# Second weights of small experts in one pass, their gate and silu moved, conversions paced by a clock model: a two-layer decoder trunk on one core

## The chip, the core and the metric

The kernel runs on one core of a Trainium2 chip. The metric is device time in microseconds from one launch, the median of three runs; for the kernel before these took 1669.72, 1660.96 and 1666.87 us. A further execution was recorded by the profiler; every row below is from that one.

The engines: TensorE (PE, with its weight loads as PEld), VectorE (DVE), ScalarE (ACT), GpSimd (POOL) and SyncE (SP), which here only issues DMAs. Each works through its own queue in the order in which the program wrote it.

## The reference, cut to what matters

Two layers; in each an attention stage and then a mixture of experts. Only the second is touched:

```python
D_MODEL, SEQ, D_EXPERT = 1024, 512, 512      # 512 tokens
N_GROUPS, EXPERTS_PER_GROUP, TOP_K = 4, 4, 2 # 16 experts, 2 per token
def _hier_moe(x, w_group, b_group, w_expert, b_expert, w1, w3, w2):
    # top-1 group, then top-2 experts of that group; gate = softmax of the two times group weight
    ...
    def expert_block(args):
        xb, e = args
        h = jax.nn.silu(xb @ w1[e]) * (xb @ w3[e])
        return h @ w2[e]
    ...   # rows times gate, summed back into their tokens
```

All weights are float32: 6.29 MB for each expert (w1 and w3 of 1024 x 512, w2 of 512 x 1024), 100.7 MB for each layer, and all sixteen experts are read. Run on the inputs, the reference routes at most 87 tokens to one expert in layer 0 and at most 142 in layer 1.

## The kernel before

A Python planner emits the whole program. In the attention stage it chooses the next step from a table of costs; in the expert stage the order is written out by hand in the loop `for e in range(NE + 1)` near the end of `trunk`. Storage is three pools: 42 pages of 128 x 1024 floats, 12 half pages (pg) and 8 PSUM banks.

**Places and kinds.** Experts are ordered at run time by their number of tokens; the first `N_FIRST` places go to experts 0, 1, ... whatever their count, so that their weights can be asked for before the routing is known. Place e takes the expert of rank `RANK[e]`. A place has a kind:

- *wide* (128 slots): rows and weights are each split into a rounded part (`hi`, ACT) and the rest (`lo`, DVE), both in fp32r, and a product is three passes: hi x hi, hi x lo, lo x hi. A wide left operand has a hi page and a lo page.
- *half* (64 slots, for the seven smallest): the left operand carries the hi of 64 tokens in columns 0 to 63 and their lo in columns 64 to 127, so a product is two passes; the two halves of the output are added after it (`folded`: a copy by ACT, an addition by DVE).
- *raw* (128 slots, ranks in `RAW`): rows and weights stay float32, a product is one float32 pass, and the weight is used as it landed.

**Blocks.** A weight block is 512 KB, one page: w1 and w3 in four blocks of two row tiles, w2 in four blocks of one. A block of w1 or w3 is two products, a block of w2 two (one for each half of the 1024 output columns). `Stream.conv_to` turns a landed block into its two parts; for a block marked `whole` it does nothing. `use(i)` first converts up to `LOOK_AHEAD` blocks beyond block i. `used(i)` frees the block and calls `ws.pump`, which emits weight loads on SP as long as more than a reserve of pages is idle (`MOE_RESERVE`, and `EX_PAGES` more while the block lies up to `EX_FROM` before a mark in place 5). A load waits on SP until the page that it was given is free.

**One place e**, in the order written: w1 of e (four blocks, into bank h1); `silu` of h1; for e = `EX_ROWS` the transposes of the rows of a possible further block; `hidden_T` of the place before (four transposes, then hi and lo of the result); w3 of e, first two blocks; w2 of e - 1, four blocks; `gated` and `scatter` of e - 1 (GpSimd adds the rows to yd); `rows_T` for e + 1; `fetch` of the rows `ROWS` places ahead; w3 of e, last two blocks; the product of silu and h3 on DVE. For half places `silu` is four steps: copy and addition (`folded`), Silu, and a multiplication by the gate; `gated` then only folds.

**Further block.** An expert with more tokens than slots gets another block of 128, run under a condition at place 5 (`further_blocks`). Its rows are fetched at the end of place 2. In this data layer 0 has none and layer 1 has one; with the new places the counts are the same.

## Time and profile before

| | us |
|---|---|
| median of three runs | 1666.87 |
| the profiled execution | 1661.48 |
| its span, first to last instruction | 1659.7 |
| expert stage of layer 0, from the first product of place 0 to the last of place 15 | 457 to 778 |
| expert stage of layer 1 | 1272 to 1625 |

The two expert stages are 321 and 353 us of the span. Times in the views are from the start of the span. In a timeline a line is a run of like instructions: start, length, engine, out<-in, count, and in brackets how long the engine had been idle before it and what ended the wait. Names are the pools' (page, pg, bank) with the numbers left out, so a line is placed by its counts: four transposes are `hidden_T`, eight are `rows_T`; a raw product is recorded as two matmuls, a wide one as three, a half one as two. Every instruction carries line 247, the helper that records them.

### The profile page before, as it was taken

To read this page: it belongs to the slowest core of one execution; us is meant where nothing else is said; L and a number is where in the kernel's file an instruction comes from. 1 tells how busy PE (TensorE), PEld (TensorE's weight loads), DVE (VectorE), ACT (ScalarE), POOL (GpSimd) and SP (SyncE) were. 2 spreads that over 40 slices of the span, in tenths; PEclk is the share of its full clock that TensorE was granted. 3 is DMA by queue.
4 is the path that set the end of the run, shared out by engine and by line. 5 is a ranking of instruction groups with operands and counts; after the bars stand their busy time and mean duration, and the time that the engine had idled before them with its cause. 6 is when DMAs were issued, how large, how long until landed. Compare 5 with 4: busy or idle time off the path is not lost. (4 is left out here: it accounts for less than half of the span.)

```text
span 1659.7 us, 22603 instructions
## 1 busy us (share of the span) xinstructions
PE 1437.5 (87%) x7604; PEld 1165.7 (70%) x7604; DVE 1097.8 (66%) x1961; ACT 873.8 (53%) x1675; POOL 336.2 (20%) x387
## 2 busy tenths in 40 slices
PE   8999999989697898987799999989696978888974
PEld 7988778877665566565699977879584655566662
DVE  4745674475886579586865546645758765597786
ACT  5444455443356577585544434555423654586772
POOL 1511110330412211111422112002213121111112
PEclk9999998999798899998789999989797989899987
DMA  8202111354299999994330102206334999599933
GB/s 255 67 1 76 53 39 39 111 196 178 102 322 336 323 324 370 360 332 143 122 96 26 45 20 90 76 8 217 133 127 151 382 309 346 187 369 363 365 131 127
DMA packets 152447, 303.59 MB, mean 183 GB/s; under 512 B 21976, under 2 KB 45224, under 8 KB 152312
## 3 DMA queue, kind: packets, MB, share of 16 engines
q1 hardware_dynamic: 138680, 269.74, 45.9%
q0 software_dynamic: 12448, 32.13, 6.9%
q8 instruction: 64, 1.05, 0.3%
q14 instruction: 71, 0.58, 0.1%
q10 hardware_dynamic: 1184, 0.08, 0.1%
HBM read 284.14 MB, written 27.33 MB: 188 GB/s over the span
## 5 line engine op out<-in xcount | busy, mean ns | idle before, releaser
L247 PE MATMUL bank<-page,page 128*128 128x512 f32 (+5 forms) x4416 | 982.8, 375 | 51.8 <-DVE page L247 30.1
L247 PEld LDWEIGHTS bank<-page,page 128*128 128x128 f32 (+2 forms) x4416 | 747.2, 202 | 198.0 <-issue 42.1
L247 DVE TENSOR_TENSOR page<-page,page 128x1024 fp32r<-128x1024 f32 (+4 forms) x462 | 517.2, 1162 | 144.1 <-ACT page L247 135.1
L247 ACT ACTIVATE page<-page 128x1024 fp32r<-128x1024 f32 (+1 forms) x438 | 420.2, 1020 | 60.0 <-DMA page<-yd 15.7
L247 PE MATMUL bank<-page,pg 128*128 128x64 f32 (+1 forms) x1408 | 320.0, 373 | 56.3 <-ACT pg L247 45.8
L247 PEld LDWEIGHTS bank<-page,pg 128*128 128x128 f32 x1408 | 244.3, 207 | 127.6 <-ACT pg L247 53.6
L247 ACT ACTIVATE page<-bank 128x256 f32<-128x256 f32 (+8 forms) x251 | 120.6, 504 | 245.0 <-PE bank L247 182.0
L247 ACT ACTIVATE pg<-bank 128x256 f32<-128x256 f32 (+6 forms) x223 | 101.6, 469 | 212.6 <-PE bank L247 207.5
L247 POOL DMA_INDIRECT yd<-page,xidx x30 | 46.6, 1554 | 474.7 <-ACT page L247 229.1
L247 DVE TENSOR_TENSOR page<-bank,page 128x256 fp32r<-128x256 f32 (+3 forms) x134 | 75.1, 594 | 76.7 <-ACT page L247 76.6
L247 PE MATMUL bank<-cid,pg 128*128 128x128 f32 (+2 forms) x500 | 85.0, 288 | 35.6 <-ACT pg L247 20.3
L247 PE MATMUL bank<-cid,page 128*128 128x128 f32 (+1 forms) x608 | 87.9, 283 | 31.6 <-DMA page<-x1d,eix 18.4
L247 POOL TENSOR_TENSOR page<-pg,pg 128x256 f32<-128x256 f32 (+1 forms) x56 | 50.3, 911 | 267.2 <-DVE pg L247 215.9
L247 PEld LDWEIGHTS bank<-cid,page 128*128 128x128 f32 (+1 forms) x608 | 72.3, 144 | 44.6 <-issue 23.0
L247 PEld LDWEIGHTS bank<-cid,pg 128*128 128x128 f32 (+2 forms) x500 | 59.0, 148 | 54.5 <-ACT pg L247 26.1
L247 ACT ACTIVATE pg<-pg 128x256 f32<-128x256 f32 (+5 forms) x146 | 68.6, 477 | 52.2 <-DVE pg L247 48.5
L247 POOL TENSOR_TENSOR page<-page,page 128x1024 f32<-128x1024 f32 (+4 forms) x32 | 63.8, 1998 | 158.7 <-ACT page L247 72.5
L247 DVE TENSOR_TENSOR pg<-bank,pg 64x512 f32<-64x512 f32 (+6 forms) x87 | 49.5, 568 | 47.8 <-ACT pg L247 46.7
L247 POOL CAST page<-page 64x512 fp32r<-64x512 f32 x48 | 29.9, 623 | 137.5 <-ACT page L247 103.3
L247 DVE COPY pg<-bank 128x256 f32<-128x256 f32 (+3 forms) x73 | 35.2, 484 | 25.6 <-PE bank L247 25.3
L247 POOL MEMSET page<- 128x1024 f32 (+1 forms) x34 | 45.8, 1347 | 16.7 <-PE bank L247 16.7
L247 ACT ACTIVATE page<-bank,gslot 128x512 f32<-128x512 f32 (+1 forms) x36 | 24.4, 686 | 40.6 <-PE bank L247 40.6
(217 smaller groups left out, 990.5 us busy)
## 6 DMA issues: line engine op xcount, KB each, us to landing
page<-in_w_dram SPq DMA_DIRECT2D x396, 512.0 KB
page<-in_w_in_dram SPq DMA_DIRECT2D x64, 512.0 KB
page<-in_w_out_dram SPq DMA_DIRECT2D x16, 512.0 KB
x1d<-page SPq DMA_DIRECT2D x8, 512.0 KB
yd<-page SPq DMA_DIRECT2D x8, 512.0 KB
page<-yd SPq DMA_DIRECT2D x8, 512.0 KB
scr<-pg POOLq DMA_DIRECT2D x16, 132.0 KB, 2.0
pg<-scr POOLq DMA_DIRECT2D x16, 132.0 KB, 4.0
```

The costliest lines, as they stand in the source:

```text
L247: r = f(*args, **kw)
```

## The change

- The w2 of half places is marked `whole`. `hidden_T` of a half place then copies 64 float32 columns on ACT (no hi and lo), a product of its w2 is one float32 pass with a left operand of 64 columns, and `gated` scales 64 rows by the gate on ACT as for the others. The multiplication of the silu by the gate and the two folds of the output go.
- Silu of a half place is written behind `hidden_T` instead of ahead of it.
- `RAW` goes from ranks 0, 3 and 6 to rank 0: two places of each layer are wide instead.
- `N_FIRST` 3, with `RANK` to match: places 1 and 2 are both wide, 13 and 14 both half.
- Conversions: at least 2 blocks ahead, up to 10 as long as the planner's clock of DVE is less than 2000 ns past its clock of PE and seven pages are idle. Loads: at most 22 landed and not yet converted; reserve 8 more pages for 12 blocks before the mark.
- Rows are fetched two places ahead of their transposes instead of one, and the rows of the further block are transposed in place 4.

```diff
-EX_ROWS = 3
+EX_ROWS = 4
-ROWS = 2
-LOOK_AHEAD = 5
-N_FIRST = 2
-RANK = (0, 1, 9, 2, 10, 3, 11, 4, 12, 5, 13, 6, 14, 7, 15, 8)
+ROWS = 3
+LOOK_AHEAD = (2, 10)
+MOE_RAW = 22
+CONV_LAG = 2000.0
+N_FIRST = 3
+RANK = (0, 1, 2, 9, 3, 10, 4, 11, 5, 12, 6, 13, 7, 14, 15, 8)
-RAW = (0, 3, 6)
+RAW = (0,)
-EX_FROM = 5
+EX_FROM = 12
-EX_PAGES = 5
+EX_PAGES = 8
...
-            return ws.add(src, k, D // k, whole=KIND[e] == "raw")
+            return ws.add(src, k, D // k, whole=KIND[e] == "raw" or KIND[e] == "half" and w is w2)
...
-                th = pg([128, 4, 128], F32 if kind == "raw" else F32R),
+                th = pg([128, 4, n]),
...
-            if kind == "raw":
+            if kind == "wide":
+                halves(th, b, slice(0, 4))
+            else:
                 nc.scalar.activation(th[0], b, AF.Copy)
-            else:
-                halves(th, b, slice(0, 4))
...
         def quarter2(ys, ht, w, j):
+            m = ht[0].shape[2]
             for n in range(2):
-                product(ys[n], [a[:, j] for a in ht], [p[:, 0, n * 512:(n + 1) * 512] for p in w], j == 0, j == 3)
+                product(ys[n][0:m], [a[:, j] for a in ht], [p[:, 0, n * 512:(n + 1) * 512] for p in w], j == 0, j == 3)
...
             if kind == "half":
                 folded(sl[0:64], h1)
-                nc.scalar.activation(sl[0:64], sl[0:64], AF.Silu)
-                nc.scalar.activation(sl[0:64], sl[0:64], AF.Copy, scale=g)
...
-        def gated(ys, g, kind="wide"):
-            yo = page([128, D])
-            for n in range(2):
-                c = slice(512 * n, 512 * n + 512)
-                if kind == "half":
-                    folded(yo[0:64, c], ys[n])
-                else:
-                    nc.scalar.activation(yo[:, c], ys[n], AF.Copy, scale=g)
+        def gated(ys, g, n=128):
+            yo = page([n, D])
+            for i in range(2):
+                nc.scalar.activation(yo[:, 512 * i:512 * i + 512], ys[i][0:n], AF.Copy, scale=g[0:n])
...
         def use(i):
-            ws.conv_to(min(i + LOOK_AHEAD, moe_q[l, NE - 1, "w2"][3]))
+            top = moe_q[l, NE - 1, "w2"][3]
+            ws.conv_to(min(i + LOOK_AHEAD[0], top))
+            while (ws.conv_i <= min(i + LOOK_AHEAD[1], top) and plan.clock["DVE"] < plan.clock["PE"] + CONV_LAG
+                   and len(page_s.idle) >= 2 + MOE_RESERVE):
+                ws.conv_to(ws.conv_i)
             return ws.parts[i]
...
-        ws.limit = moe_q[l, NE - 1, "w2"][3] + 1
+        ws.limit, ws.max_raw = moe_q[l, NE - 1, "w2"][3] + 1, MOE_RAW
...
             ht = hidden_T(prev, KIND[e - 1]) if e else None
             if e < NE:
+                if KIND[e] == "half":
+                    nc.scalar.activation(sl[0:64], sl[0:64], AF.Silu)
                 use_13(e, "w3", h3, range(2))
```

The order on ACT in layer 0, where a wide place is followed by a half one. Before (place 10): conversions (page<-page), the copy of `folded` (pg_8521<-bank), Silu, the gate, and then the hi part of `hidden_T` (pg_8527).

```order
L247 ACTIVATE page_8501<-page_8123 128x1024
L247 ACTIVATE page_8511<-page_8133 128x1024
L247 ACTIVATE pg_8521<-bank_8476 64x512
L247 ACTIVATE pg_8521<-pg_8521 64x512
L247 ACTIVATE pg_8521<-pg_8521,gslot 64x512
L247 ACTIVATE pg_8527<-bank_8529 128x512
L247 ACTIVATE page_8536<-page_8143 128x1024
```

Now, at the same spot (place 9; the copy is pg_8343<-bank, the hi part pg_8347):

```order
L249 ACTIVATE page_8323<-page_8021 128x1024
L249 ACTIVATE page_8333<-page_8041 128x1024
L249 ACTIVATE pg_8343<-bank_8302 64x512
L249 ACTIVATE pg_8347<-bank_8349 128x512
L249 ACTIVATE pg_8343<-pg_8343 64x512
L249 ACTIVATE page_8361<-page_8053 128x1024
```

The hi part of `hidden_T` no longer stands behind the Silu, and the multiplication by gslot is gone.

The order on DVE at the same spots. Before: two folds of the output of place 8 (page_8425<-bank), two lo parts of `rows_T` (128x4x64), two conversions, the product with h3 of place 9 (pg_8338), four conversions, the addition of `folded` (pg_8521) and the lo part of `hidden_T` (pg_8528).

```order
L247 TENSOR_TENSOR page_8425<-bank_8374,page_8425 64x512
L247 TENSOR_TENSOR page_8433<-bank_8434,page_8433 128x4x64
L247 TENSOR_TENSOR page_8433<-bank_8441,page_8433 128x4x64
L247 TENSOR_TENSOR page_8455<-page_8097,page_8453 128x1024
L247 TENSOR_TENSOR page_8465<-page_8109,page_8463 128x1024
L247 TENSOR_TENSOR pg_8338<-pg_8338,bank_8340 128x512
L247 TENSOR_TENSOR page_8479<-page_8111,page_8477 128x1024
L247 TENSOR_TENSOR page_8493<-page_8113,page_8491 128x1024
L247 TENSOR_TENSOR page_8503<-page_8123,page_8501 128x1024
L247 TENSOR_TENSOR page_8513<-page_8133,page_8511 128x1024
L247 TENSOR_TENSOR pg_8521<-bank_8476,pg_8521 64x512
L247 TENSOR_TENSOR pg_8528<-bank_8529,pg_8527 128x512
```

Now:

```order
L249 TENSOR_TENSOR page_8263<-bank_8264,page_8263 128x4x64
L249 TENSOR_TENSOR page_8263<-bank_8271,page_8263 128x4x64
L249 TENSOR_TENSOR page_8291<-page_7969,page_8289 128x1024
L249 TENSOR_TENSOR pg_8177<-pg_8177,bank_8179 128x512
L249 TENSOR_TENSOR page_8305<-page_7983,page_8303 128x1024
L249 TENSOR_TENSOR page_8309<-page_7993,page_8307 128x1024
L249 TENSOR_TENSOR page_8325<-page_8021,page_8323 128x1024
L249 TENSOR_TENSOR page_8335<-page_8041,page_8333 128x1024
L249 TENSOR_TENSOR pg_8343<-bank_8302,pg_8343 64x512
L249 TENSOR_TENSOR pg_8348<-bank_8349,pg_8347 128x512
```

Ahead of the product with h3 (pg_8177) stands one conversion instead of two, and the folds are gone; between that product and the addition there are four conversions in both.

The order on SP at the end of the attention stage of layer 0. Before: the last weight loads of places 0 and 1, the eight stores of x1d and yd (four token tiles each), then the read of the routing order, behind which all other loads stand.

```order
L247 DMA page_4322<-in_w_dram 128x2x512
L247 DMA x1d_295<-page_3725 128x1024
L247 DMA yd_298<-page_3725 128x1024
L247 DMA x1d_295<-page_3723 128x1024
L247 DMA x1d_295<-page_3721 128x1024
L247 DMA yd_298<-page_3723 128x1024
L247 DMA x1d_295<-page_3719 128x1024
L247 DMA yd_298<-page_3721 128x1024
L247 DMA yd_298<-page_3719 128x1024
L581 TENSOR_LOAD order
```

Now, the end of that stretch, with the last five of twelve further loads:

```order
L249 DMA x1d_296<-page_3724 128x1024
L249 DMA yd_299<-page_3724 128x1024
L249 DMA page_4574<-in_w_dram 128x1024
L249 DMA x1d_296<-page_3722 128x1024
L249 DMA x1d_296<-page_3720 128x1024
L249 DMA page_4610<-in_w_dram 128x1024
L249 DMA page_4612<-in_w_dram 128x1024
L249 DMA page_4681<-in_w_dram 128x2x512
L249 DMA yd_299<-page_3722 128x1024
L249 DMA page_4686<-in_w_dram 128x2x512
L249 DMA yd_299<-page_3720 128x1024
L583 TENSOR_LOAD order
```

Twelve loads that do not need the order stand ahead of it, some of them between the stores.

## Rows read from the trace of the kernel before

**Rows 1.** The page: the span, and PE's busy time, share of the span and instructions.

```profile
span 1659.7 us, 22603 instructions
...
PE 1437.5 (87%) x7604; PEld 1165.7 (70%) x7604; DVE 1097.8 (66%) x1961; ACT 873.8 (53%) x1675; POOL 336.2 (20%) x387
```

**Rows 2.** The waits of PE in the expert stage of layer 0 (457 to 770 us): who waited for whom, us in total, times, the longest.

```profile
PE bank L247 <- ACT pg L247: 21.0, 7, 4.2
PE bank L247 <- DMA page<-x1d,eix: 9.5, 1, 9.5
PE bank L247 <- DMA page<-in_w_dram: 2.7, 1, 2.7
```

**Rows 3.** The same in the expert stage of layer 1 (1272 to 1620 us).

```profile
PE bank L247 <- ACT pg L247: 20.4, 7, 4.2
...
PE bank L247 <- DMA page<-x1d,eix: 8.9, 1, 8.9
```

**Rows 4.** The timeline of PE early in the expert stage of layer 0: w2 of the raw place 0 and the transposes after it; w2 of the wide place 1 and the transposes after it; the list and the transposes of the further block; w2 of the wide place 3 and the transposes after it.

```profile
480.13 7.03 PE L247 MATMUL bank<-page,pg 128*128 128x512 f32 x16
487.00 1.04 PE L247 MATMUL bank<-cid,page 128*128 128x128 f32 x8
...
499.62 7.63 PE L247 MATMUL bank<-page,pg 128*128 128x512 f32 x24 [2.90 <-ACT pg L247]
507.09 1.03 PE L247 MATMUL bank<-cid,page 128*128 128x128 f32 x8
...
509.87 0.44 PE L247 MATMUL bank<-pg,pg 128*128 128x1 bf16 x12
...
525.41 1.94 PE L247 MATMUL bank<-cid,page 128*128 128x128 f32 x8 [9.53 <-DMA page<-x1d,eix]
527.28 0.69 PE L247 MATMUL bank<-cid,pg 64*128 64x64 f32 x4
...
548.89 8.64 PE L247 MATMUL bank<-page,pg 128*128 128x512 f32 x24 [3.26 <-ACT pg L247]
557.37 1.04 PE L247 MATMUL bank<-cid,page 128*128 128x128 f32 x8
```

**Rows 5.** The timeline of PE around places 8 to 10 of layer 0: w2 of the half place 8, `rows_T`, the last w3 blocks of the wide place 9, w1 of the half place 10, its first w3 blocks, w2 of place 9, `rows_T`.

```profile
648.12 3.89 PE L247 MATMUL bank<-page,pg 128*128 128x512 f32 x16
651.86 1.03 PE L247 MATMUL bank<-cid,page 128*128 128x128 f32 x8
652.65 2.98 PE L247 MATMUL bank<-page,page 128*128 128x512 f32 x12
656.45 3.92 PE L247 MATMUL bank<-page,page 128*128 128x512 f32 x16 [0.83 <-DVE page L247]
...
660.57 2.10 PE L247 MATMUL bank<-page,page 128*128 128x512 f32 x8
666.83 7.62 PE L247 MATMUL bank<-page,pg 128*128 128x512 f32 x24 [4.16 <-ACT pg L247]
674.28 1.03 PE L247 MATMUL bank<-cid,page 128*128 128x128 f32 x8
```

**Rows 6.** The timeline of DVE in the same stretch: two folds and two lo parts of `rows_T`, two conversions, the product with h3 of place 9, four conversions, the addition of `folded`, the lo part of `hidden_T`.

```profile
654.79 1.94 DVE L247 TENSOR_TENSOR page<-bank,page 64x512 f32<-64x512 f32 x4
656.65 2.34 DVE L247 TENSOR_TENSOR page<-page,page 128x1024 fp32r<-128x1024 f32 x2
658.92 0.67 DVE L247 TENSOR_TENSOR pg<-pg,bank 128x512 f32<-128x512 f32 x1
659.52 4.62 DVE L247 TENSOR_TENSOR page<-page,page 128x1024 fp32r<-128x1024 f32 x4
664.06 0.68 DVE L247 TENSOR_TENSOR pg<-bank,pg 64x512 f32<-64x512 f32 x1
666.81 0.69 DVE L247 TENSOR_TENSOR pg<-bank,pg 128x512 fp32r<-128x512 f32 x1 [2.07 <-ACT pg L247]
```

**Rows 7.** The timeline of ACT in the same stretch: Silu of place 10, the multiplication by its gate, the hi part of `hidden_T` of place 9.

```profile
664.77 0.63 ACT L247 ACTIVATE pg<-pg 64x512 f32<-64x512 f32 x1 [3.76 <-DVE pg L247]
665.43 0.72 ACT L247 ACTIVATE pg<-pg,gslot 64x512 f32<-64x512 f32 x1
666.18 0.60 ACT L247 ACTIVATE pg<-bank 128x512 fp32r<-128x512 f32 x1
```

**Rows 8.** Stretches of layer 0, PE, PEld, DVE, ACT and POOL busy us (x instructions), granted TensorE clock, DMA share, GB/s: from w2 of place 5 to w2 of place 7, from there to w2 of place 9, and from w2 of place 13 to near the end of the stage.

```profile
592.00:629.20 37.20, 32.25 (x137) 23.11 (x137) 32.35 (x35) 29.88 (x39) 7.34 (x6) 1.00 1.04 374
629.20:666.80 37.60, 32.64 (x144) 25.62 (x144) 34.10 (x36) 30.78 (x40) 7.35 (x6) 0.95 1.03 371
...
740.30:775.00 34.70, 29.44 (x117) 23.08 (x118) 29.00 (x35) 24.85 (x30) 4.80 (x5) 0.84 0.25 67
```

**Rows 9.** The timeline of PE in layer 1: `rows_T` just ahead of the further block, and the first products behind it.

```profile
1388.60 1.04 PE L247 MATMUL bank<-cid,page 128*128 128x128 f32 x8
...
1425.70 7.38 PE L247 MATMUL bank<-page,page 128*128 128x512 f32 x24 [0.87 <-PEq L2094]
```

**Rows 10.** The timeline of SP (DMA issues) from 444 to 461 us: the last stores of yd, and the first weight load behind the read of the order.

```profile
444.53 1.24 SPq L247 DMA_DIRECT2D yd<-page  x2
460.62 0.41 SPq L247 DMA_DIRECT2D page<-in_w_dram  x1
```

**Rows 11.** Groups of instructions over the whole span, shapes kept apart: the lo part of a conversion on DVE (busy us, mean ns of one | idle before, and what ended it).

```profile
L247 DVE TENSOR_TENSOR page<-page,page 128x1024 fp32r<-128x1024 f32 x410 | 489.1, 1237 | 140.3 <-ACT page L247 131.7 <-issue 6.4 <-DMA page<-in_w_dram 0.3
```

More of the change, by code (lines that the diff above doesn't have):

```diff
@@ L2020, in folded, with silu @@
             nc.vector.tensor_tensor(o, b[0:64], o, op=OP.add)
-        def silu(h1, kind="wide", g=None):
+        def silu(h1, kind="wide"):
             sl = pg([128, 512])
@@ L2045, in scatter @@
             nc.gpsimd.indirect_dma_start(out=yd[l], out_offset=bass.IndirectOffsetOnAxis(ap=idx[0:n], axis=0),
-                                         in_=yo[0:n], in_offset=None, bounds_check=T - 1, oob_is_err=False,
+                                         in_=yo, in_offset=None, bounds_check=T - 1, oob_is_err=False,
                                          compute_op=OP.add)
@@ L2243, in trunk @@
                 use_13(e, "w1", h1, range(4))
-                sl = silu(h1, KIND[e], gslot[0:64, e:e + 1])
+                sl = silu(h1, KIND[e])
                 if e == NE - 1:
@@ L2265, in trunk @@
                 if e < NE:
-                    scatter(gated(ys, gslot[:, e - 1:e], KIND[e - 1]), xidx[:, e - 1:e], SLOTS[e - 1])
+                    scatter(gated(ys, gslot[:, e - 1:e], SLOTS[e - 1]), xidx[:, e - 1:e], SLOTS[e - 1])
                 if e == NE - 1:
```

## The prediction

> **What bounds the kernel now.** I read the page first: PE is busy 1437.5 us of a span of 1659.7, 87% [rows 1]. What is left for a change that touches only the expert stages is PE's idle time there, PE's own work there, and the clock it runs at. So I went on to PE's waits in the two stages. In layer 0 the reader sees 21.0 us of waits in which ACT came last on a pg, in 7 waits of up to 4.2 us, one of 9.5 us for the rows of the further block, and one of 2.7 us for a weight [rows 2]; in layer 1 the same picture with 20.4 and 8.9 us [rows 3]. PE waits for ACT, hardly ever for a weight.
>
> Then the timelines of one such place. PE ends the first w3 blocks of place 10 at about 660.57 + 8 x 0.234 = 662.4 and starts w2 of place 9 at 666.83, after 4.16 us [rows 5]. ACT shows why: the Silu of place 10 waits 3.76 us for DVE, then come Silu, the multiplication by the gate, and only then the hi part of `hidden_T` [rows 7]. What Silu waited for is the addition of `folded`, which DVE starts at 664.06 behind four conversions [rows 6]. These began late because the product with h3 of place 9 started at 658.92, though PE had ended its last products at 652.65 + 2.98 = 655.6: DVE was still at two folds, two lo parts and two conversions [rows 5, 6]. DVE is 34.1 of 37.6 us busy there [rows 8]. So the path is PE's products, then DVE's queue, then ACT's, then PE again.
>
> A wait costs more than itself. After 2.90, 3.26 and 4.16 us of waiting the next 24 passes took 7.47, 8.48 and 7.45 us from start to start, where 24 x 0.234 = 5.6 is full speed [rows 4, 5]. The granted clock is 1.00 in the stretch that has only short waits and 0.95 in the next one [rows 8]; PE dropped from 2.4 to 1.2 GHz for a part.
>
> DMA is the other candidate: share 1.03 to 1.04 at 371 to 374 GB/s in those stretches [rows 8]. But from 740.3 to 775 it moved only 67 GB/s x 34.7 us = 2.3 MB, some four blocks, while PE still multiplied the 22 blocks from w2 of place 13 on. So 18 blocks, 9.4 MB or 25 us at 371 GB/s, lay loaded ahead of PE. Loads fill the pages and then go at PE's pace.
>
> **The change part by part.** Prices per pass come from start-to-start times: a float32 product (487.00 - 480.13) / 8 = 0.859 us [rows 4]; an fp32r pass (651.86 - 648.12) / 16 = 0.234 us [rows 5].
>
> *More work on PE.* Two places of each layer go from raw to wide: 24 x 0.859 = 20.6 against 72 x 0.234 = 16.8, so -7.6 for both. Seven half places take w2 raw: 8 x (0.859 - 2 x 0.234) = +3.1 each, +21.9. The trace has no float32 product with 64 columns on the left. It could not be cheaper than what it replaces by any row here (0.468, which would take 22 us off for each layer) nor dearer than the raw one; the number of columns that stream through is the same 512, so I take 0.859. Sum +14.3 for a layer, **+28.7** in all. PE carries this in full.
>
> *The wide-to-half waits.* Of the 14 waits on ACT [rows 2, 3] ten are of this kind; the rest are at raw-to-half places, which no longer exist, and one at the end. All of it is 41.4 us, and ten times 1.9 us of slow clock (the middle of 1.9, 2.9 and 1.8) is 19: **-60.4**. What takes their place: ACT makes the hi part at once, and the lo part is late next, behind the addition on DVE. With DVE as late as now it ends at 664.06 + 0.68 + 0.69 = 665.4; PE needs it for its third pass, at 662.4 + 0.5 = 662.9, so 2.5 us would stay. But the folds (two of the four in 1.94) and one of two conversions (1.17) go from ahead of the product with h3 [rows 6], which is some 2.2 us, and twenty instead of 24 conversions stand in a pair of places (4 x 1.155 = 4.6 of 34.1 busy). That leaves 0.3. Between 0 and 2.5 I take 0.8, the size of the waits on DVE that are seen now [rows 5]; there are six such places in a layer: **+9.6**. At that length no clock is lost [rows 8].
>
> *The further block's rows.* PE reached them 15.1 us after the list was done, having waited 9.5 [rows 4]; now they are transposed in place 4, with place 3, w2 of place 2 and w1 of place 4 in between: 7.5 + 5.6 + 5.6 + 1.6 for transposes = 20.3 us. Covered by 5 us. **-18.4**, and -2.1 for the slow transposes behind (1.87 where 0.79 is usual [rows 4, 5]). Without that cover it would come back one for one.
>
> *Conversions paced by the clock.* Now DVE may be only two blocks ahead. Half blocks take PE 4 x 0.234 = 0.94 us and DVE 4.62 / 4 = 1.155 from start to start [rows 6], 1.24 by itself [rows 11]. Over a half place without w2, DVE has 8 x 1.155 + 3.4 of other work = 12.6 against 8.6 on PE; the 4.0 us missing must be earned during raw w2 (6.9 us of PE, no conversion). Between 0 and 4.0 us for each of 14 half places; DVE has 28 to 30 us of work in a pair of 34 us, so near the lower end: 0.5, **+7**.
>
> *Loads.* SP gets twelve loads ahead of the read of the order, five of them between the stores of x1d and yd. Now SP ends its stores at 445.8 and idles until 460.6 [rows 10]; the stores could slip by ten us before the fetch of places 1 and 2 or the read felt it. Nothing waited for a weight at the start, so the twelve loads gain nothing either: 0. The 13 pages kept idle for a block before the mark may cost lead: **+4**, from 0 to 27 (below). The second row fetch ahead hides under POOL's 20% [rows 1]; no row of these waits shows x1d,xidx, so 0. Around the further block of layer 1 (37 us from 1388.6 to 1425.7 [rows 9]) the conditions hardly change: 0, give or take 7.
>
> *Sum:* 28.7 - 60.4 + 9.6 - 18.4 - 2.1 + 7 + 4 = **-31.6**. The profiled execution took 1661.5, so 1629.9; the median of the three runs is 5.4 above it: **1635**.
>
> **The rivals.** *DMA becomes the bound.* A pair of a wide and a half place needs 371 GB/s x 37.6 us = 13.95 MB. PE's pair becomes 16.8 + 14.4 + 2.4 for transposes + 1.3 of waits = 34.9. If the lead is gone after place 5, five pairs in each layer go at 37.6: +27 instead of +4, **1658**. Against it: the lead of 25 us is more than the 5 x 2.7 = 13.5 that a layer would eat. For it: pages held back for twelve blocks, and a share that is at 1.03 already [rows 8].
>
> The Trainium skill, "DMA: Bandwidth & Descriptors", Specifications, gives a core about 358 GB/s of HBM; by that the pair would take 39.0 us, the ten pairs 41 us more than PE, and the time would be 1672. The rows show 371 and 374 here, so the trace does not agree, and the Trainium skill, "HBM Reference", Specifications (TRN2), says that a core streaming alone measures about 425, by which (32.8 us) DMA would not bind at all.
>
> *The lo part stays late.* If DVE is not earlier, 2.5 us stay at twelve places, with or without 1.9 us of slow clock: +20 to +43, **1655 to 1678**. It decides once the lo part is more than two us late; the two fewer jobs on DVE speak against it.
>
> *The other side: DVE's two-block lead is too short.* Place: w1 and w3 of every half place. Price: up to 4.0 us at 14 places, 56 instead of 7: **1684**, slower. It decides if the planner's clock of DVE runs far enough past PE's that nothing is converted ahead during raw w2. Against: the old order left PE only waits of 0.8 on DVE's pages while DVE had more work.
>
> *The change does not do what it says:* stores or fetches pushed back by loads that wait for pages on SP, so that PE waits at places 1 and 2: ten us in each layer, **1655**.
>
> **How the numbers follow.** Forecast 0.68; DMA 0.10; lo part 0.10; two-block lead 0.08; stores 0.04. With all the small terms at 0 the sum is -52 (1614), and 7 less at the further block: low end **1608**. The upper end takes in the DMA case, the stores and the cheap half of the late lo part: **1662**; some 0.12 lies above, 0.05 below. About 0.5% (8 us) is what a measurement of this kernel tells from no change. Faster by more: the forecast, and about half of the DMA, lo-part and stores cases: 0.79. Within: 0.12. Slower: the two-block lead and little else, 0.09.
>
> **What would show it.** Right: PE's waits on ACT pg fall from 41 us to under 10; the wait for x1d,eix is gone; w2 of half places takes 6.9 us for 16 matmuls; granted clock near 1.00 in the pairs, which take 34 to 35 us. Wrong: pairs still at 37 us with PE waiting for in_w (DMA), waits of 2 us and more on DVE pg ahead of a wide w2 (lo part), or many waits of half a us and more on DVE page in half places (lead). A w2 of half places far from 6.9 us would move the first term itself.

## The result, and the profile after

The changed kernel takes 1621.84 us (median of four runs, 1616.86 to 1625.82) where the kernel before, run beside it, took 1668.30: a ratio of 0.9724, interval 0.9674 to 0.9775. The forecast was 1635, from 1608 to 1662. The profiled execution took 1625.72 against 1661.48 before: -35.8 where the sum gave -31.6. It is near the slowest of its four runs, that of before near the fastest of its, so the medians lie 46.5 apart.

The page of the profile after, to be held against [rows 1]: PE's busy time has grown by 18 us and the span has fallen by 36.

```profile
span 1623.4 us, 22651 instructions
...
PE 1455.7 (90%) x7700; PEld 1160.8 (72%) x7700; DVE 1068.1 (66%) x1919; ACT 859.7 (53%) x1657; POOL 327.4 (20%) x388
```

PE's waits in the expert stage of layer 0 (455 to 760 us), then of layer 1 (1250 to 1590), both below: us in total, times, the longest. Against [rows 2, 3] the 21.0 and 20.4 us on ACT pg are 0.7 and 0.7, and no wait names x1d,eix or in_w. New in layer 0 are a long wait on ACT page and one for PE's sequencer; new in layer 1 is one called "issue" (idle time for which the profile shows no cause). The long wait on ACT page in layer 1 had its like before, as the first line here shows, which is of layer 1 in the kernel before. All of these lie around place 5.

```profile
PE bank L247 <- ACT page L247: 8.7, 2, 7.1
```

```profile
PE bank L249 <- DVE page L249: 5.9, 8, 1.3
PE bank L249 <- ACT page L249: 4.6, 1, 4.6
...
PE bank L249 <- PEq L2091: 2.9, 1, 2.9
PE bank L249 <- ACT pg L249: 0.7, 1, 0.7
```

```profile
PE bank L249 <- DVE page L249: 8.9, 12, 1.2
PE bank L249 <- ACT page L249: 8.6, 3, 6.3
PE bank L249 <- issue: 4.1, 1, 4.1
...
PE bank L249 <- ACT pg L249: 0.7, 1, 0.7
```

The timeline of PE in places 9 and 10 of layer 0, to be held against [rows 5]: `hidden_T` of the wide place, the first w3 blocks of the half one, the wide w2, `rows_T`, the wide place's w1, and the w2 of a half place.

```profile
631.50 0.60 PE L249 MATMUL bank<-cid,pg 128*128 128x128 f32 x4
631.86 2.10 PE L249 MATMUL bank<-page,page 128*128 128x512 f32 x8
633.79 6.06 PE L249 MATMUL bank<-page,pg 128*128 128x512 f32 x24
639.70 1.03 PE L249 MATMUL bank<-cid,page 128*128 128x128 f32 x8
...
646.26 2.80 PE L249 MATMUL bank<-page,page 128*128 128x512 f32 x11 [0.68 <-DVE page L249]
...
652.34 7.08 PE L249 MATMUL bank<-page,pg 128*64 128x512 f32 x16
659.35 1.09 PE L249 MATMUL bank<-cid,page 128*128 128x128 f32 x8
```

The wide w2 starts without the 4.16 us of waiting that it had, and takes 639.70 - 633.79 = 5.91 us from start to start where 24 passes at 0.234 are 5.6. A w2 of a half place takes 659.35 - 652.34 = 7.01 us.

DVE in the same stretch (to [rows 6]): the product with h3, four conversions, and the addition of `folded` with the lo part. The product starts 0.18 us after PE ended, where it was 3.3 us late.

```profile
628.07 0.69 DVE L249 TENSOR_TENSOR pg<-pg,bank 128x512 f32<-128x512 f32 x1 [0.18 <-PE bank L249]
628.68 4.63 DVE L249 TENSOR_TENSOR page<-page,page 128x1024 fp32r<-128x1024 f32 x4
633.22 1.27 DVE L249 TENSOR_TENSOR pg<-bank,pg 64x512 f32<-64x512 f32 x2
```

ACT there (to [rows 7]): the copy of `folded` and the hi part of `hidden_T` follow PE at once, and the Silu, still waiting for DVE, no longer has a part of `hidden_T` behind it.

```profile
631.70 1.22 ACT L249 ACTIVATE pg<-bank 64x512 f32<-64x512 f32 x2 [1.28 <-PE bank L249]
633.93 0.63 ACT L249 ACTIVATE pg<-pg 64x512 f32<-64x512 f32 x1 [1.01 <-DVE pg L249]
```

A pair of a wide and a half place by windows (to [rows 8], columns as there): 35.2 us instead of 37.6, PE busy 34.4, DVE 28.2 instead of 34.1, clock 1.00, DMA share 1.03.

```profile
633.79:668.97 35.18, 34.36 (x145) 23.69 (x144) 28.22 (x30) 26.58 (x34) 7.32 (x6) 1.00 1.03 368
```

Place 5 is where the change lost. PE in layer 0 around the condition: `rows_T`, 14 matmuls, then single products. ACT's first conversion behind the condition, and the scatter of place 4 on POOL:

```profile
558.06 1.03 PE L249 MATMUL bank<-cid,page 128*128 128x128 f32 x8
562.02 5.08 PE L249 MATMUL bank<-page,page 128*128 128x512 f32 x14 [2.93 <-PEq L2091]
571.72 0.80 PE L249 MATMUL bank<-page,page 128*128 128x512 f32 x1 [4.62 <-ACT page L249]
572.98 5.74 PE L249 MATMUL bank<-page,page 128*128 128x512 f32 x17 [0.46 <-DVE page L249]
578.65 0.46 PE L249 MATMUL bank<-cid,pg 64*128 64x64 f32 x4
...
570.61 1.06 ACT L249 ACTIVATE page<-page 128x1024 fp32r<-128x1024 f32 x1 [10.69 <-DMA yd<-page,xidx]
...
559.23 1.94 POOL L249 DMA_INDIRECT yd<-page,xidx  x1 [13.03 <-DMA page<-in_w_dram]
```

From 558.06 to 578.65 PE takes 20.6 us for 8.3 us of work (32 passes and eight transposes). No term of the sum stood for the 12.3 us lost there.

**How runs are compared below.** A *step* runs on PE's timeline from the `hidden_T` that stands in one place to that in the next, a *stage* from the first `hidden_T` of a layer to its last. The stages are what the change touches. The rest of the span is the same work of PE in every kernel and came out between 1030 and 1044 us, so the stages tell small differences more sharply than the medians; but they come from one profiled execution each, and so have no interval. "Step 5" is that from place 5 to 6 in layer 0; "block" is the two steps around the executed further block in layer 1. All in us; ratios are to the kernel before, run beside each. One of the six executions of mark_ahead took 3562.68 us, for which no run shows a cause; the median of the other five is 1614.17.

| kernel | both stages | step 5 | block | median | ratio |
|---|---|---|---|---|---|
| before | 619.6 | 21.1 | 54.5 | 1668.30 | |
| after | 579.6 | 29.9 | 59.6 | 1621.84 | 0.967 to 0.978 |
| only_silu | 600.2 | 24.6 | 60.4 | 1643.50 | 0.983 to 0.991 |
| silu_ahead | 591.5 | 30.8 | 59.3 | 1633.84 | 0.974 to 0.984 |
| w2_split | 621.0 | 30.7 | 58.9 | 1658.66 | 0.992 to 0.997 |
| rows_early | 594.6 | 30.8 | 57.4 | 1635.09 | 0.977 to 0.986 |
| two_fixed | 585.0 | 24.3 | 54.2 | 1628.41 | 0.973 to 0.981 |
| reserve_old | 589.7 | 32.9 | 66.8 | 1632.65 | 0.976 to 0.983 |
| five_ahead | 573.4 | 25.1 | 56.1 | 1607.87 | 0.961 to 0.969 |
| raw_three | 568.4 | 19.8 | 50.6 | 1606.30 | 0.961 to 0.970 |
| other_pages | 569.0 | 23.6 | 55.2 | 1611.38 | 0.964 to 0.970 |
| mark_ahead | 575.5 | 27.2 | 53.0 | 1616.46 | 0.967 to 0.973 |
| raw_pages | 575.1 | 19.7 | 57.8 | 1617.41 | 0.968 to 0.974 |
| five_pages | 566.7 | 20.8 | 56.8 | 1611.99 | 0.964 to 0.974 |

### The profile page after: what moved, and what is told of

Read it like the earlier page. It is cut to its first block, busy times and chain, and to the rows that moved or that the text cites. A ratio compares the mean times of both kernels' runs of the same rounds, so it can differ in the third digit from the quotient of the medians.

```text
span 1623.4 us, 22651 instructions
## 1 busy us (share of the span) xinstructions
PE 1455.7 (90%) x7700; PEld 1160.8 (72%) x7700; DVE 1068.1 (66%) x1919; ACT 859.7 (53%) x1657; POOL 327.4 (20%) x388
## 4 chain that ended last, share of the span: by engine, by line
PE 25%; DMA 10%; DVE 9%; issue 7%; ACT 4%; SPq 0%; DVEq 0%; ACTq 0%; POOLq 0%
PE bank L249 25%; DMA page<-in_w_dram 5%; DVE page L249 4%; ACT page L249 3%; DMA yd<-page,xidx 2%; DVE pg L249 2%; DVE st L249 1%; DMA page<-in_w_in_dram 1%; ACT pg L249 1%; DVE nst L249 1%; DVE bst L249 1%; DMA yd<-page,eix 0%; DMA page<-yd 0%; DVE sel L249 0%; SPq L249 0%
## 5 line engine op out<-in xcount | busy, mean ns | idle before, releaser
L249 PEld LDWEIGHTS bank<-page,page 128*128 128x128 f32 (+2 forms) x4480 | 761.2, 203 | 199.0 <-DVE page L249 50.8
L249 DVE TENSOR_TENSOR page<-page,page 128x1024 fp32r<-128x1024 f32 (+3 forms) x454 | 508.5, 1164 | 168.0 <-ACT page L249 159.9
L249 ACT ACTIVATE page<-page 128x1024 fp32r<-128x1024 f32 (+2 forms) x430 | 411.8, 1018 | 53.6 <-DMA page<-in_w_in_dram 12.4
L249 PE MATMUL bank<-page,pg 128*128 128x64 f32 (+2 forms) x1440 | 338.0, 377 | 17.9 <-ACT page L249 5.2
L249 PEld LDWEIGHTS bank<-page,pg 128*128 128x128 f32 (+1 forms) x1440 | 223.6, 189 | 122.1 <-issue 65.7
L249 ACT ACTIVATE pg<-bank 128x256 f32<-128x256 f32 (+5 forms) x223 | 101.7, 470 | 218.4 <-PE bank L249 216.4
L249 ACT ACTIVATE page<-bank 128x256 f32<-128x256 f32 (+7 forms) x227 | 108.0, 495 | 180.3 <-PE bank L249 115.9
L249 DVE TENSOR_TENSOR page<-bank,page 128x256 fp32r<-128x256 f32 (+3 forms) x114 | 63.7, 582 | 92.2 <-ACT page L249 92.1
L249 PE MATMUL bank<-cid,page 128*128 128x128 f32 (+1 forms) x608 | 88.0, 283 | 10.8 <-DVE page L249 5.3
L249 ACT ACTIVATE page<-bank,gslot 128x512 f32<-128x512 f32 (+2 forms) x64 | 42.9, 685 | 72.0 <-PE bank L249 71.9
L249 POOL CAST page<-page 64x512 fp32r<-64x512 f32 x48 | 29.9, 623 | 136.3 <-ACT page L249 102.8
L249 DVE COPY pg<-bank 128x256 f32<-128x256 f32 (+3 forms) x73 | 35.1, 484 | 28.3 <-PE bank L249 28.2
L249 DVE TENSOR_TENSOR pg<-bank,pg 64x512 f32<-64x512 f32 (+5 forms) x77 | 45.3, 600 | 5.4 <-ACT pg L249 4.3
```

The lines of the kernel that those rows point to most:

```text
L249: r = f(*args, **kw)
```

## The experiments

**The theory first.** The waits went because the hi part no longer stands behind Silu on ACT *and* DVE comes sooner to the fold; the further block's rows are covered by a place more; and place 5 lost because pages are held back there. The rivals are that one of the two, ACT's order or DVE's relief, did it alone. The last part of the theory fell, and was replaced half-way.

### The order on ACT alone (only_silu)

The kernel before, with Silu and the gate written behind `hidden_T`:

```diff
                 folded(sl[0:64], h1)
-                nc.scalar.activation(sl[0:64], sl[0:64], AF.Silu)
-                nc.scalar.activation(sl[0:64], sl[0:64], AF.Copy, scale=g)
...
             if e < NE:
+                if KIND[e] == "half":
+                    nc.scalar.activation(sl[0:64], sl[0:64], AF.Silu)
+                    nc.scalar.activation(sl[0:64], sl[0:64], AF.Copy, scale=gslot[0:64, e:e + 1])
                 use_13(e, "w3", h3, range(2))
```

> The kernel before with one part of the change alone: Silu of half places, and the multiplication by the gate with it, written behind hidden_T. The weights, kinds and conversions are as before. Theory (the order on ACT and the relief of DVE each take a share): ACT makes the hi part without waiting for the fold, but DVE reaches the lo part 2.5 us after PE wants it, as worked out in the prediction; so of the 41 us of waits and 19 of slow clock some 12 to 25 us go, 1643 to 1655, and PE's waits now name DVE pg. Rival 1 (the order alone is the cause): all 41 + 19 go, about 1607. Rival 2 (DVE's queue alone is the cause): within 5 us of the kernel before, with the same waits put down to DVE.

1643.50 us: within the theory's bounds, at their low end; both rivals fall. The timeline of PE at the same spot as in [rows 5]:

```profile
657.83 0.62 PE L247 MATMUL bank<-page,pg 128*128 128x512 f32 x2
660.71 4.62 PE L247 MATMUL bank<-page,pg 128*128 128x512 f32 x12 [2.27 <-DVE pg L247]
```

The waits of PE in layer 0 (457 to 765 us):

```profile
PE bank L247 <- DVE pg L247: 18.0, 9, 4.2
PE bank L247 <- DMA page<-x1d,eix: 10.6, 1, 10.6
PE bank L247 <- DVE page L247: 3.7, 6, 0.8
```

The hi part is in time, two passes run, and the third waits 2.27 us for the lo part: the wait has changed its engine and kept half of its size. The prediction had 2.5 us for just this, "with DVE as late as now".

### DVE's relief alone (silu_ahead)

The changed kernel with Silu back ahead of `hidden_T`:

```diff
                 folded(sl[0:64], h1)
+                nc.scalar.activation(sl[0:64], sl[0:64], AF.Silu)
...
-                if KIND[e] == "half":
-                    nc.scalar.activation(sl[0:64], sl[0:64], AF.Silu)
```

> The changed kernel with the Silu of half places back ahead of hidden_T; the multiplication by the gate stays away. It separates the two reasons for which the 41 us of PE waits on ACT pg can have gone. Theory (both: DVE reaches the addition of the fold earlier because its queue holds two folds, a lo part and two conversions of w2 less, and the hi part no longer stands behind the Silu): the addition starts at 633.22 in place 9 of layer 0, Silu takes 0.63, so the hi part would end 1.3 to 1.4 us later than now at each of 12 places where a half place follows a wide one; PE waits 1 to 1.6 us there: +17, with slow clock behind it up to +25. Rival 1 (the order on ACT alone did it): the old waits of 2.9 to 4.2 us come back at 12 places, +40 to +60. Rival 2 (the relief on DVE alone did it): PE waits for nothing new, 0 to +3.

Stages +11.9, medians +12.0. The wait is as the theory had it; the timeline of PE in place 9:

```profile
640.73 6.01 PE L249 MATMUL bank<-page,pg 128*128 128x512 f32 x24 [1.28 <-ACT pg L249]
```

A pair by windows, columns as in [rows 8]:

```profile
600.50:637.00 36.50, 34.50 (x146) 23.55 (x144) 28.36 (x30) 26.64 (x34) 7.02 (x6) 1.00 1.00 347
```

The total is under its 17, since five such places in a layer lost the 1.4 us and the last steps got 1.3 back, and no clock was lost: 1.00 in the pair. Side by side, the wait ahead of a wide w2 is 4.16 us before, 2.27 with the order alone, 1.28 with the relief, and none with both. Neither part alone would have done.

### Half places' w2 in two passes again (w2_split)

```diff
-            return ws.add(src, k, D // k, whole=KIND[e] == "raw" or KIND[e] == "half" and w is w2)
+            return ws.add(src, k, D // k, whole=KIND[e] == "raw")
...
-            if kind == "wide":
-                halves(th, b, slice(0, 4))
-            else:
+            if kind == "raw":
                 nc.scalar.activation(th[0], b, AF.Copy)
+            else:
+                halves(th, b, slice(0, 4))
...
+                    nc.scalar.activation(sl[0:64], sl[0:64], AF.Copy, scale=gslot[0:64, e:e + 1])
```

(and the two folds of the output again).

> The changed kernel with the second weights of half places in two fp32r passes again: converted, hi and lo parts in hidden_T, the outputs folded, the gate multiplied into the silu (behind hidden_T). PE has 14 x (7.05 - 8 x 2 x 0.234) = 46 us less work in all; DVE gets four conversions (4 x 1.155), a lo part and two folds (1.94 with the hi side) more in each pair: 28.2 + 4.6 + 0.7 + 1.4 = 34.9 us of work in a pair that now takes 35.2. Theory (raw w2 pays because it takes DVE off the path): pairs stay at 35 to 37 us with DVE full and the addition late again, so 0 to +15 us in all. Rival 1 (raw w2 was only PE work bought for nothing; the order on ACT made the gain): pairs fall to 32 us, 20 to 40 us faster than after. Rival 2 (DMA is the bound of the pairs): no change at all in the pairs, 35 us with DMA at 1.03, and DVE under 33 busy with gaps on PE for landed blocks.

None of the three sizes came out: the stages are 41.4 us longer, although PE has 46 us less to do. A pair by windows, columns as in [rows 8]:

```profile
597.16:635.82 38.66, 34.31 (x145) 25.20 (x144) 34.16 (x37) 30.81 (x39) 14.68 (x7) 0.96 0.96 344
```

The waits of PE in layer 0 (455 to 775 us):

```profile
PE bank L249 <- DVE page L249: 16.9, 27, 1.2
PE bank L249 <- ACT page L249: 16.3, 7, 4.6
```

The theory's direction holds: DVE is at 34.2 us and PE waits for it. But it comes in layer 0 as 27 waits of up to 1.2 us for pages that DVE has yet to write, and 7 on ACT's, which is how the prediction described its rival of the two-block lead. So the raw w2 seems to pay for more than the late fold: it also gives DVE and ACT the 7 us in which a lead of two blocks is made up. That is argued and not shown apart: how the 41 us divide between the weight and the lead (this kernel with five blocks ahead) was not run.

### The further block's rows in place 3 (rows_early)

```diff
-EX_ROWS = 4
+EX_ROWS = 3
```

> The changed kernel with the rows of the further block transposed in place 3 again, as before. Theory (the list ends later than PE reaches place 3's end, so PE waits for the rows): the wait of 9.5 and 8.9 us is back, and some 2 us of slow transposes, so +18 to +22 us. Rival 1 (the wider places 1 and 2 take PE longer, so that the list is done in time now): the wait is under 3 us, +0 to +6. Rival 2 (the time is given back later since DMA goes on while PE waits, and the loads' lead then saves it): +5 to +12, with the pairs behind it shorter than 35.1 us.

Stages +15.0, medians +13.3: the theory's kind, but less than its 18 to 22. The transposes wait again, 7.28 us in layer 0 and 6.73 in layer 1 instead of 9.5 and 8.9, and run slowly behind it (1.73 us to the next start, where 0.79 is usual):

```profile
517.65 1.94 PE L249 MATMUL bank<-cid,page 128*128 128x128 f32 x8 [7.28 <-DMA page<-x1d,eix]
519.38 1.06 PE L249 MATMUL bank<-cid,pg 128*128 128x128 f32 x4
```

That step is 25.6 and 25.0 us in the two layers where it is 16.4: +17.8, just under the theory's size. Layer 1 gives 2.2 back in its block.

### Two fixed places (two_fixed)

```diff
-N_FIRST = 3
-RANK = (0, 1, 2, 9, 3, 10, 4, 11, 5, 12, 6, 13, 7, 14, 15, 8)
+N_FIRST = 2
+RANK = (0, 1, 9, 2, 10, 3, 11, 4, 12, 5, 13, 6, 14, 7, 15, 8)
```

> The changed kernel with two places fixed instead of three and the old ranks, so that place 2 is half and the two half places stand elsewhere. Theory (nothing waited for a weight at the stage's start, so twelve more early loads gain nothing): 0, give or take 5. Rival 1 (the early loads bring the first products forward or keep the lead): +8 to +15. Rival 2 (the order of the half places around the further block decides how long the list stays covered): the wait for its rows is back in part, +5 to +18, seen in place 4.

Stages +5.4, the medians' intervals overlap. Step 5 is shorter (a half place stands ahead of it), other steps longer. It decides little: that the third fixed place is worth up to some five us, by the order of the kinds, and nothing by early loads that a wait would name.

### The pages held back (reserve_old)

```diff
-EX_FROM = 12
-EX_PAGES = 8
+EX_FROM = 5
+EX_PAGES = 5
```

> The changed kernel with the pages kept idle ahead of the further block as before: 5 pages for 5 blocks instead of 8 for 12. In the profile after, PE lost 12.3 us around place 5 of layer 0 (20.6 us from the rows_T at 558.06 to the hidden_T at 578.65 for some 8.3 us of work, with 4.62 us of waiting for a page of ACT's and 2.93 us for its own sequencer), where the kernel before lost 3.9, and 24.9 us around the further block of layer 1, where it lost 20. Theory (the idle pages cost the loads their lead, and the pages come back as bulk behind the mark): both places go back to what they were, 8.4 + 4.9 = 13 us less, so about 1609, ratio to after 0.992. Rival 1 (the loss belongs to the condition and to the yd stores on SP, whatever the reserve): 0, the same rows at place 5. Rival 2 (the reserve is what lets the further block's pages be given without a wait): slower by up to 10 us in layer 1, none in layer 0.

Slower by 10.1 in the stages, all of it at place 5 (+3.0) and at the block (+7.2). **My theory of place 5 falls**, and rival 2 is nearest: the larger reserve helps there. In layer 1 ACT's first conversion in the branch that runs waits 11.49 us for a weight, where it waits 4.33 in the changed kernel. (By the count further down, the kernel before lost 5.6 us at place 5 and not 3.9, and layer 1 lost 3.2 more and not 4.9.)

### Two runs that were faster for another reason (five_ahead, raw_three)

```diff
-LOOK_AHEAD = (2, 10)
+LOOK_AHEAD = (5, 5)
```

> The changed kernel with conversions five blocks ahead always, as before, instead of two to ten by the planner's clock. Theory (DVE has 28 us of work in a pair of 35, so the rule of when to convert matters little): within 5 us of after, since four conversions stand ahead of the addition of the fold either way. Rival 1 (the clock rule is what keeps the addition and the product with h3 early): waits on DVE or ACT pg come back at 12 places, +10 to +30. Rival 2 (the clock rule costs: each pair shows one wait of 0.65 to 0.69 us on a page of DVE's): these go, 5 to 10 us faster.

```diff
-RAW = (0,)
+RAW = (0, 3, 6)
```

> The changed kernel with ranks 0, 3 and 6 raw again: two places of each layer go from three fp32r passes to one float32 product. Theory (PE carries a product's time in full): 24 x 0.859 against 24 x 3 x 0.234 is +3.8 us a place, +15 us for four, less what DVE's and ACT's idle time there gives; so +10 to +16. Rival 1 (PE is not the bound of those pairs, DMA at 1.03 is): 0 to +4. Rival 2 (without conversions DVE and ACT get a rest that shortens the waits at place 5): faster by up to 5.

five_ahead: stages -6.2 and the median 14 us lower, outside the theory's 5. The pairs are 35.4 instead of 35.2, so the clock rule is worth 0.2 us a pair, as the theory had it; the gain is elsewhere, above all 4.8 at step 5 and 3.5 at the block. raw_three: stages -11.2, where +10 to +16 was expected. A pair with a raw place does cost 1.8 more (37.0 to 35.2), but step 5 gives 10.1 back and the block 9.0. PE behind the condition, in five_ahead and then in raw_three:

```profile
559.12 9.10 PE L249 MATMUL bank<-page,page 128*128 128x512 f32 x32 [1.93 <-PEq L2091]
572.21 0.46 PE L249 MATMUL bank<-cid,pg 64*128 64x64 f32 x4 [3.99 <-DVE pg L249]
```

```profile
555.69 2.09 PE L249 MATMUL bank<-page,page 128*128 128x512 f32 x8
559.52 5.72 PE L249 MATMUL bank<-page,page 128*128 128x512 f32 x24 [1.74 <-DVEq L2091]
```

Both have 32 matmuls of converted blocks there, and after has 14. (A raw place 4 needs no conversions, which leaves DVE and ACT time for those of place 6.) So the second theory: **behind the condition hardly a conversion is done for some ten us, and PE lives on what was converted ahead.** In after there is none; five_ahead gets one done and raw_three two before ACT waits 6.3 and 6.5 us. Why it stops stands in the program. The first conversion behind the branches, with what it waits for, in after and in other_pages below:

```
ACTIVATE page_7752<-page_5416 128x1024 [waits DMAHW2_49,DMAHW3_49,DMAHW1_49,DMAHW4_49,DMAHW0_49,DMAHW5_49,DMASW0_49,DMAHW6_49,DVE_49,DMAHW7_49,PE_49,Activation_49]
ACTIVATE page_7752<-page_5416 128x1024 [waits DMAHW7_49]
```

The page that it writes has also been given out inside the branches. That no branch is taken does not help: the program waits for twelve semaphores (nine of DMA, three of engines), and so for every transfer under way, the scatter of place 4 last. The planner gives out the page that has been idle longest, inside the branches and behind them alike, so they meet.

### Other pages behind the condition (other_pages)

```diff
+KEPT = 3
...
             n_ex = extra.pop("n")
+            kept = sorted(page_s.idle, key=lambda n: page_s.free_at[n])[:KEPT]
+            for n in kept:
+                page_s.idle.remove(n)
             state = plan.state()
...
             plan.restore(state)
+            for n in page_s.idle:
+                page_s.free_at[n] += 20000.0
+            page_s.idle.extend(kept)
```

> The changed kernel, in which the branches of the further block may use all idle pages but the three that came free longest ago, and the pages that they may use are given out late behind it. In the program after, the first conversion behind the condition (ACT 570.61 in layer 0, after 10.69 us) writes a page that the branches use too, and it waits on eleven DMA and engine semaphores at once: on all transfers issued ahead of the condition, the scatter of place 4 (559.23 to about 570.6) last. PE has 14 matmuls of converted blocks then (5.08 us) and waits. Here no conversion behind the condition waits on more than one load. Theory (those pages are the cause of the loss at place 5): ACT's and DVE's waits of 10.7 and 10.8 us are under 2 us, the step from the hidden_T of place 5 to that of place 6 goes from 29.9 to 18 to 21 us in layer 0, and the two steps around the executed block of layer 1 from 59.6 to 50 to 57, so 12 to 20 us in all, 1602 to 1610. Rival 1 (SP's own wait at the condition, 11.5 us, starves PE next): PE waits for landed blocks instead, gain under 5. Rival 2 (the condition's own cost on the engines' sequencers): no change.

Stages -10.6 (-6.1 and -4.5), ratio 0.9671 against 0.9724: the cause is shown, and its size is somewhat below the 12 to 20; ACT still waits 4.74 us where under 2 was expected. (The semaphores are twelve, not eleven.) The timelines of PE and ACT at the condition:

```profile
563.57 6.57 PE L250 MATMUL bank<-page,page 128*128 128x512 f32 x21 [3.55 <-PEq L2095]
570.46 2.83 PE L250 MATMUL bank<-page,page 128*128 128x512 f32 x11 [0.32 <-DVE page L250]
...
565.59 1.06 ACT L250 ACTIVATE page<-page 128x1024 fp32r<-128x1024 f32 x1 [4.74 <-ACTq L2095]
```

ACT's 10.69 us on the scatter are gone. What is left of the loss, 23.6 against the usual 17.7, is for the most part the sequencers' own, as rival 2 had it for the whole: 3.55 us on PE and 4.74 on ACT to get past the condition. Its nine branches are nested, each inside the one before, so that in layer 0, where the first is not taken, none of the others is reached.

### More converted ahead (mark_ahead)

```diff
             top = moe_q[l, NE - 1, "w2"][3]
-            ws.conv_to(min(i + LOOK_AHEAD[0], top))
+            at = moe_q[l, EX_RUN, "w3"][2]
+            near = (i - (at - 14)) // 2 if at - 14 <= i < at else 0
+            ws.conv_to(min(i + LOOK_AHEAD[0] + near, top))
```

> The changed kernel with conversions that run ahead of PE by one block more for every second block over the fourteen blocks ahead of the condition, up to eight; the pages are as in the change. It is the other way to take the same loss away: the long wait stays, but PE has 8 blocks to work on. Theory (the loss at place 5 is the wait less what is converted ahead: 3.5 blocks after, 6 with five blocks ahead, 4 to 5 us of PE between them): the step at place 5 goes from 29.9 to 19 to 22 us in layer 0, and the two steps of layer 1 from 59.6 to 50 to 54, so 13 to 18 us in all less up to 3 for products and folds that come later on DVE ahead of it. Rival 1 (the gain with five blocks ahead came from the rule, not from the condition): no change at place 5. Rival 2 (conversions ahead of the condition push the scatter back by as much): a gain of 3 to 6.

Stages -4.1: the block as expected (53.0), step 5 not (27.2). Rival 2 shows in part: the extra conversions stand ahead of the fold and of the scatter, so PE waits 2.39 us for DVE ahead of the condition, where after had 0.76, and 3.96 for DVE at it.

```profile
551.93 6.92 PE L249 MATMUL bank<-page,pg 128*128 128x512 f32 x22 [2.39 <-DVE pg L249]
...
566.51 7.33 PE L249 MATMUL bank<-page,page 128*128 128x512 f32 x24 [3.96 <-DVEq L2091]
```

### Raw places once the wait is gone (raw_pages), and both covers (five_pages)

other_pages with one line more each, first raw_pages, then five_pages:

```diff
-RAW = (0,)
+RAW = (0, 3, 6)
```

> The changed kernel with both: ranks 0, 3 and 6 raw, and the pages of the further block's branches kept from what follows. With raw ranks alone the time fell by 15 us though PE has 15 us more of products; the steps between places show that raw places cost 1.8 us each there, and that the step at place 5 alone fell by 10 us in each layer. Theory (raw places helped only since they left DVE and ACT time to convert 6 blocks ahead of the condition): with the condition's wait gone their price is what is left, 4 x 1.8 = 7 us, so 5 to 9 us slower than the kernel with the pages alone. Rival 1 (raw places are better in themselves, DVE and ACT relieved): 8 to 15 us faster than the pages alone, about 1595. Rival 2 (both help at place 5 in part): within 3 us of each other.

```diff
-LOOK_AHEAD = (2, 10)
+LOOK_AHEAD = (5, 5)
```

> The changed kernel with five blocks ahead and with the pages of the further block's branches kept from what follows. By the steps between places, five blocks ahead took 3.7 us from the stage of layer 0 and 2.5 from that of layer 1 and the pages 6.1 and 4.5. Theory (both are cover for the same stretch behind the condition, and five blocks ahead saves 2 us more at the last three places of each layer): the wait of 6.31 us on ACT behind the condition goes, the step at place 5 of layer 0 is 19 to 22 where 25.1 and 23.6 stood, the stages together 560 to 566 us from the first hidden_T to the last, where 573.4 and 569.0 stood, so 4 to 8 us faster than the pages alone, 1603 to 1608. Rival (the waits come back on DVE pg and the pairs cost 0.2 us more each): within 2 us of the pages alone, 1610.

raw_pages is 6.1 us slower in the stages than other_pages, as its theory had it: raw places helped only through the condition. five_pages has step 5 at 20.8 and the shortest stages of all, 566.7, but 2.3 us below other_pages instead of 4 to 8, since the executed block got longer (37.5 where 34.2 stood); its median of 1611.99 is that of the pages alone. Its rival was right on the time. Which of five_ahead, raw_three and other_pages is the fastest their intervals don't tell; their medians are 10 to 16 us below the change's, and none of their executions was as slow as its fastest, though their ratios overlap with its ratio.

## Why the prediction came out

The forecast of 1635 was 13 us too high: 4 of them in the sum, the rest in how the two profiled executions stand to their medians. The mechanism came out as forecast but for the further block. That the sum came so close is in part luck, for terms that were too large stood against a loss that no term had. The two stages by windows, columns as in [rows 8], before and then after:

```profile
476.90:771.30 294.40, 253.36 (x1027) 182.49 (x1025) 221.23 (x244) 203.46 (x260) 58.58 (x46) 0.93 0.90 317
1292.70:1618.00 325.30, 274.84 (x1103) 198.65 (x1101) 237.02 (x258) 218.20 (x276) 59.01 (x44) 0.92 0.86 306
...
477.20:752.10 274.90, 258.91 (x1075) 176.90 (x1073) 205.75 (x230) 192.78 (x247) 53.29 (x44) 0.98 0.92 323
1279.00:1583.70 304.70, 279.75 (x1151) 191.51 (x1149) 221.50 (x244) 207.37 (x263) 53.24 (x42) 0.98 0.88 312
```

PE's idle time in the stages, their length less its busy time, fell from 91.5 to 40.9 us, and its busy time grew by 10.5 us. Term by term:

- **What bounds the kernel:** right. The path was PE, then DVE's queue, then ACT's, then PE; only_silu and silu_ahead show each engine's share.
- **More work on PE, +28.7:** right. The w2 of a half place measured 7.01 us where 6.87 was forecast: +2 in all, so 30.7. In the time of a pair, wide for raw gave 1.8 us a place and not 3.8, in part because a wide w2 takes 5.91 and conversions are waited for in its place.
- **The wide-to-half waits, -60.4:** right. Inside the stages the waits on ACT pg went from 40.7 us to none (the 0.7 us in each list after lies behind the last `hidden_T`). PE's busy time grew by 10.5 us for 30.7 us of work, so some 20 us of slow passes went, by difference, where the sum had 19 here and 2.1 at the rows. The granted clock rose from 0.93 and 0.92 to 0.98.
- **The lo part, +9.6:** too large. In the pairs PE has no wait for it, and a wide w2 takes 5.91 - 5.6 = 0.3 us a place too long instead of 0.8.
- **The further block's rows, -20.5:** right in mechanism. The 18.4 us of waits are gone; by rows_early this is worth 15.0 in the new order.
- **Conversions paced by the clock, +7:** about right. PE's short waits away from place 5 and from the last `hidden_T` went from 4.9 to 10.8 us, with one of 0.68 us in each pair.
- **Loads, +4:** no wait of PE in the stages names a weight, so near 0; ACT waits for weights there only in the branch that runs, 9.4 us (10.7 before). The pairs run at 361 to 368 GB/s and DMA share 1.02 to 1.03 without binding. That is above the 358 of the Trainium skill, "DMA: Bandwidth & Descriptors", Specifications, by which the prediction's 1672 was worked out; the measurement decides.
- **Not in the sum:** at the last `hidden_T` of each layer PE waited 4.55 us on DVE pg before and 1.77 after, which took off 5.6 us.
- **Around the further block, "the conditions hardly change: 0, give or take 7":** this step failed. From `rows_T` to `hidden_T`, the time above PE's work went from 5.6 us (574.65 to 588.22 before) to 12.3 in layer 0 and up by 3.2 in layer 1 (46.9 to 50.4 for 0.3 more of work): +10, of which 6.7 are waits and the rest slow passes. The prediction weighed only how many pages are kept, which reserve_old shows to be a help. What changed is the lead at the condition: 14 matmuls are three blocks, the 24 that PE had there before were six, and the wait behind it is in both kernels (there ACT waited 4.61 us for the same scatter). The two-block lead was a rival for the half places; it came true at the one spot where conversions stop.

Together 30.7 - 40.7 - 20.2 - 18.4 + 5.9 - 5.6 + 6.7 and 1.6 of waits too short for the list give the -40.0 of the stages; the rest of the span was 3.7 us longer.

The prediction held two prices for one pair. Term by term it came out at 3.1 - 4.16 - 1.9 + 0.8 + 0.5 = -1.7, and by its PE work, in the DMA rival, at 37.6 to 34.9 = -2.7. It measured 37.6 to 35.2, which is -2.4. The list added the new waits, but did not take off the 0.83 us on a page of DVE's that the pair had before [rows 5], where the new 0.68 now stands.

## What to carry to other kernels

A steady part of a kernel gives the price of a change twice, as a list of waits and as a period less the busiest engine's work; work out both, and look for what is missing where they differ: here the list had a new wait, but not the old one in whose place it came. Where a chain runs through several queues, undoing one link at a time tells what each is worth: here 4.16 us of waiting fell to 2.27 and to 1.28 by one link, and to nothing only by both. A cheaper lead is safe in the steady part and has to be looked at where the supply stops: behind a condition, storage that its branches use carries their waits even when no branch is taken.

## What the runs showed of the hardware

A float32 product with 64 columns on the left takes what one with 128 takes: 0.876 us against 0.859. At the condition of layer 0, none of whose branches runs, PE stood idle for 0.15 to 3.84 us (raw_pages, reserve_old; 2.93 in after) and ACT for 1.32 to 5.17 (five_pages, two_fixed) in waits that the profile puts down to the engine's own sequencer. In w2_split PE has 46 us less to do and the two stages are 41 us longer; in layer 0 PE then waits 33 us for pages that DVE and ACT have yet to write.
